# A hybrid attention and retention layer on one core: values freed by one cast and one subtraction, context units ahead of the values, summed weights made ahead, output weights in wider steps

## The chip, the cores and the metric

The kernel runs on one core of one Trainium2 chip. The metric is the device time of one execution in microseconds (us), as the median of several runs. The core has a matrix engine (TensorE, PE in the profile), a vector engine (VectorE, DVE), a scalar engine (ScalarE, ACT), GpSimd (POOL) and SyncE (SP), which issues most DMA transfers; ScalarE has a DMA queue of its own. Each engine takes its instructions in the order of the program and waits at each for what it needs.

## The reference

One backbone layer over 2048 latent tokens and 256 context tokens of width 1024, in float32:

```
h_lat = rmsnorm(x)*(1+scale)+shift;  h_ctx = rmsnorm(ctx)*(1+scale_c)+shift_c
[na_q|na_k|na_v|na_g|r_q|r_k|r_v|r_g] = h_lat @ w_in        # 8 groups of 512 columns
k_ctx, v_ctx, rk_ctx, rv_ctx          = the same columns of h_ctx @ w_in
o_na  = neighbourhood attention of 8 heads (8 x 16 window + all context keys, one softmax)
o_ret = forward + backward retention of 4 heads, scans started from the context's state
y     = concat(o_na*silu(na_g), head_rmsnorm(o_ret)*silu(r_g)) @ w_out
out   = rmsnorm(x + gate*y)
```

## The kernel before

Every float32 factor is held as a rounded part (hi, made by a cast on ScalarE) and a remainder (lo, made by a subtraction on VectorE or GpSimd), and each product is three products: hi by hi, hi by lo, lo by hi. The 2048 tokens of `h_lat` lie in four blocks of 512 (`blk[0]` to `blk[3]`, tiles `hhi` and `hlo`), the context in `blk[4]` (`chi`, `clo`). The order of the work is written out by hand; the part around the change goes so:

- Windows 0 to 4 compute the attention keys for one block each. A table `PLAN` says at which step each preparation stands. `spill_step` writes a piece of 512 KB of `h` to memory (`hS`); blocks 2 and 3 are spilled in windows 3 and 4, blocks 0 and 1 in the first Strassen part.
- A *unit* is a product of 256 tokens with 256 columns: 48 matmuls (line 365). `w_split` cuts 256 columns of weights from a raw tile `st` into `whi` and `wlo` (ScalarE line 336, line 338), two buffers each; `load_w` loads the next raw tile (SP, line 176), and two raw tiles fit.
- `u_v` is the unit of the attention values. It frees its result with two casts on ScalarE (line 405) and two subtractions on VectorE (line 406) into a tile `o` (two buffers), and writes eight pieces to `vB` (line 415), four from ScalarE's queue and four from SP's.
- `values` runs eight `u_v` units for two blocks. Between their steps `h_sums` makes sums of the blocks (`T`, lines 525 to 565), and after the fifth unit `w_sums` begins the first set of summed weights.
- `strassen` then runs six *sets* of 256 columns (gates and queries) over two blocks. A set is Strassen's scheme with seven products of 12 matmuls (line 623), in the order a11, a12, s4, a22, s2, s3, s1. `w_sums` makes the seven weights of the next set meanwhile (`cut`: ScalarE line 580, GpSimd line 581; sums on VectorE, lines 589 to 592) in functions `p0` to `p3`, which `step` calls after products 2, 4, 6 and 7; each writes into the buffers `whi` and `wlo` of the current set once that set's products have read them.
- The hooks of `strassen` are called at the same steps. In the second part they hold the work on the output weights: `wo_open`, eight `wo_gate` (a row of the gate: VectorE), `wo_row` (TensorE line 696), eight `wo_mul` (a multiplication on VectorE, line 700; two casts on ScalarE, line 704; two subtractions on GpSimd, line 705; four stores `woS` from ScalarE's queue, line 707; the next load `wraw` from SP, line 686).
- In the order of time: windows; two `u_v` units for the context; values of blocks 0 and 1; Strassen for 0 and 1; reload of blocks 3 and 2 from `hS` (16 loads, lines 756 and 760) beside four context units (`u_rk`, `u_rv`); values of blocks 3 and 2; Strassen for 2 and 3; a split of the first weights for the *fill* (retention units that go between attention steps); four fill units while the first head's data load; attention with fill; retention and output.

Of the kernel before, what the change touches and what calls it, by code (L numbers as in the profile page):

```python
# [11 lines left out]
F32R = mybir.dt.float32r  # L12
# [6 lines left out]
P = 128  # L19
# [63 lines left out]
def hybrid_kernel(ctx: ExitStack, tc: tile.TileContext, a: dict, out: bass.AP):  # L83
# [53 lines left out]
    def defer(n, fn):  # L137
        later.append([n, fn])
# [187 lines left out]
    def w_raw(c0):  # L326
        return st_halves(a["w_in"][:, c0:c0 + WG])
# [70 lines left out]

    def u_v(w, c0, tp):
        pm = yield from tokform(w, tp)  # L400
        vt = op.tile([P, 2, 2, 2, P], F32R, name="o")
        pv = pm.rearrange("p (t h e d) -> p t h e d", t=2, h=2, e=2)
        for e in range(2):
            hs, ls = slice(64 * e, 64 * e + 64), slice(64 - 64 * e, 128 - 64 * e)
            nc.scalar.copy(vt[:, :, :, e, hs], pv[:, :, :, e, :])
            nc.vector.tensor_tensor(vt[:, :, :, e, ls], pv[:, :, :, e, :], f(vt)[:, :, :, e, hs], ALU.subtract)
        s, o = (c0 - 1024) // WG, f(vt).rearrange("p t h e d -> p t (h e d)")
        if tp == 8:
            store(vS[s].rearrange("(t p) h d -> p t (h d)", p=P), o)
            return  # L410
        for e, j in enumerate(VORD):
            k0, cw = CWIN[j]
            dst = vB[s][:4 * cw, tp, e, :].rearrange("(t r c) d -> r c t d", t=2, r=2)
            for r, q in enumerate((nc.scalar, nc.sync)):
                defer(1 + r, lambda q=q, dst=dst[r], src=o[64 * r + k0:64 * r + k0 + cw]: q.dma_start(dst, src))
# [42 lines left out]
    for name, *args in LOADS:  # L458
        lds[name](*args)
    acts = dict(sq=squares, cs=lambda *i: colsum(*i), rs=lambda i: (rstd(i), spread_copy(i)), sp=lambda *i: spread(*i),  # L460
                mu=lambda i, u: spread_mul(i, (u,)), ab=prep_ab, hl=prep_hl, blk=alloc_blk, x=load_x, w=lambda: wr.append(w_raw(1024)),
                w2=lambda: load_w(), s=ada_split, m=ada_mm, ar=ada_row, af=ada_fin, p=prep_first,
                ws=lambda g: w01.append(w_split(wr[g], lo=WSL[g])))
    w01 = []
# [25 lines left out]
    def window(b):  # L490
        units = [u_k(w01, 512 + 256 * g, ct, b) for g in range(2) for ct in range(2)]
        left = [KC] * 4
        for n, u in enumerate(STEPS if b == 0 else [u for u in range(4) for _ in range(KC)]):
            if b == 4 and n == 16:
                wr.append(w_split(wr[2]))
            next(units[u])
            left[u] -= 1
            run_acts(32 * b + n)
            if b > 2 and n % 4 == 3:
                spill_step()  # L500
            if not left[u]:
                for _ in units[u]:
                    pass
                tick()
# [65 lines left out]
    def w_sums(rw):  # L570
        cut2 = lambda t: t.rearrange("p k w -> p (k w)").rearrange("p (s h k c) -> p s h k c", s=2, h=2, k=KH)
        a11, a21 = rw[0][:, :, 0:P], rw[0][:, :, P:WG]
        a12, a22 = rw[1][:, :, 0:P], rw[1][:, :, P:WG]
        W, tl = {}, {}

        def cut(key, n, s, r):
            if n not in tl:
                tl[n] = cut2(wa.tile([P, KC, WG], F32R, name=("whi", "wlo")[n % 2]))
            t = W[key] = tl[n][:, s]
            nc.scalar.copy(t[:, 0], r)  # L580
            nc.gpsimd.tensor_tensor(t[:, 1], r, f(t)[:, 0], ALU.subtract)  # L581

        def p0():
            cut("a11", 0, 0, a11)
            cut("a12", 0, 1, a12)

        def p1():
            cut("a22", 1, 0, a22)
            nc.vector.tensor_tensor(a22, a21, a22, ALU.add)
            nc.vector.tensor_tensor(a21, a11, a21, ALU.subtract)  # L590
            nc.vector.tensor_tensor(a11, a22, a11, ALU.subtract)
            nc.vector.tensor_tensor(a12, a12, a11, ALU.subtract)
# [12 lines left out]
    def plain_next(res):  # L605
        def p1():
            res.append(w_split(wcur.pop(0)))

        return [None, None, p1, None]

    def w_set(c0, W, T, A, B, ahead, hooks):
        isq = c0 < 512
# [28 lines left out]
        def step(n):  # L641
            tick()
            if ahead[n]:
                ahead[n]()
            if hooks:
                h = hooks.pop(0)
                if h:
                    h()

        V = nc.vector.tensor_tensor  # L650
# [76 lines left out]
    def values(ws, bb, hs, W):  # L727
        ahead = [None] * 4
        vu = [(w, c0, tp) for w, c0 in zip(ws, (1024, 1280)) for b in bb for tp in (2 * b, 2 * b + 1)]
        y = 0  # L730
        for n, (w, c0, tp) in enumerate(vu):
            for _ in u_v(w, c0, tp):
                y += 1
                if hs and y % 5 == 0:
                    hs.pop(0)()
            tick()
            if n == 4:
                W, ahead = w_sums(wcur.pop(0))
                ahead[0]()
        while hs:  # L740
            hs.pop(0)()
        ahead[2]()
        ahead[3]()
        return W

    load_w()
    w0, w1 = wr[3], w_split(wcur.pop(0))
    load_w()
    for w, c0 in ((w0, 1024), (w1, 1280)):
        unit(u_v(w, c0, 8))  # L750
    T = []
    W = values((w0, w1), (0, 1), h_sums(T, 0, 1), None)
    mid = []
    strassen(T, 0, 1, W, [spill_step] * 24, mid)
    for d in reload_parts(3):
        nc.sync.dma_start(*d)
    (wk0,) = mid
    load_w()
    for d in reload_parts(2):
        nc.sync.dma_start(*d)  # L760
    wk1 = w_split(wcur.pop(0))
    load_w()
    unit(u_rk(wk0, 2560, 8))
    wk2 = w_split(wcur.pop(0))
    load_w()
    unit(u_rk(wk1, 2816, 8))
    wk3 = w_split(wcur.pop(0))
    load_w()
    unit(u_rv(wk2, 3328, 8))
    w0 = w_split(wcur.pop(0))  # L770
    load_w()
    unit(u_rv(wk3, 3072, 8))
    w1 = w_split(wcur.pop(0))
    load_w()
    T = []
    W = values((w0, w1), (3, 2), h_sums(T, 2, 3), None)
    g = lambda k: lambda: wo_gate(k)
    m = lambda k: lambda: wo_mul(k)
    seq = [wo_open] + [g(k) for k in range(8)] + [None, wo_row] + [m(k) for k in range(8)]
    wo_steps = []  # L780
    for n, e in enumerate(seq):
        wo_steps += [e, None] if n in (2, 4, 6, 8) else [e]
    last = []
    strassen(T, 2, 3, W, wo_steps, last)
    w_next = last + [w_split(wcur.pop(0))]
    flush()

# [754 lines left out]
```

## Time and profile before

| | before |
|---|---|
| median of 3 runs | 1489.48 us (1488.07 to 1491.04) |
| the profiled execution's own time | 1491.74 us |
| its span | 1489.9 us |
| mean granted TensorE clock | 0.955 |
| TensorE busy | 1343.9 us (90%) |
| VectorE, ScalarE, GpSimd busy | 797.9, 594.5, 639.9 us |
| moved by DMA | 295.63 MB, mean 198 GB/s |

The profile is of one execution. The page gives busy times and the busy share in 40 slices of the span; a table of stretches gives busy time, granted clock and DMA share from one time to another; the timeline lists instructions with start, duration, and in brackets how long the engine was idle just before and what ended that. Matmuls overlap a little, so the distance from one start to the next tells their pace better than the duration.

### The profile page before, as it was taken

The page shows a single profiled execution, that of the slowest core. Times are in us where ns is not written, and L with a number is a line of the kernel's source. Part 1 is how long each engine was busy: PE and PEld are TensorE (multiplying, and loading weights), DVE is VectorE, ACT ScalarE, POOL GpSimd, SP SyncE. Part 2 cuts the span into 40 slices and gives each one's busy share as a digit, 9 for nine tenths or more (in the row PEclk, how much of TensorE's full clock was granted, in tenths as well). Part 3 has the DMA queues.
Part 4 walks back from the last instruction along what each step waited for, and adds up shares of the span by engine and source line. Part 5 has one row for each costly group of instructions (what it writes and reads, how often), then busy time and mean ns, then how long its engine had stood idle before and what let it go on. Part 6 is the DMA issues. An engine that isn't in the chain of part 4 may idle for free.

```text
span 1489.9 us, 23084 instructions
## 1 busy us (share of the span) xinstructions
PE 1343.9 (90%) x8236; PEld 1169.6 (79%) x8236; DVE 797.9 (54%) x1424; ACT 594.5 (40%) x1257; POOL 639.9 (43%) x593
## 2 busy tenths in 40 slices
PE   6999896999795889648999999999999989999997
PEld 2477795777694667448989988988999879888886
DVE  5776173334146353433777677777664554344435
ACT  5444122323322223224555654555564233333332
POOL 5342424433543434553545434435544134444442
PEclk9999997999797899779999999999999999999999
DMA  9445945455944534659776778997744898655533
GB/s 319 155 149 170 341 126 164 147 212 181 374 125 126 160 110 167 233 198 248 225 189 177 195 207 262 262 252 190 199 140 145 277 282 257 209 179 170 173 114 127
DMA packets 231764, 295.63 MB, mean 198 GB/s; under 512 B 17633, under 2 KB 172385, under 8 KB 230626
## 3 DMA queue, kind: packets, MB, share of 16 engines
q1 hardware_dynamic: 195842, 230.44, 51.9%
q10 hardware_dynamic: 35808, 63.72, 12.1%
q8 instruction: 66, 1.08, 0.3%
q14 instruction: 48, 0.39, 0.1%
HBM read 196.57 MB, written 97.52 MB: 197 GB/s over the span
## 4 chain that ended last, share of the span: by engine, by line
PE 44%; DMA 5%; DVE 4%; issue 3%; POOL 2%; ACT 2%; ACTq 0%; SPq 0%; DVEq 0%; POOLq 0%
PE mm L365 10%; PE mm L1386 10%; PE sS L947 4%; PE mm L354 4%; PE tr L974 3%; PE po L995 3%; PE mm L1109 2%; PE tr L976 2%; PE po L997 2%; DMA v<-rvS 1%; PE mm L1298 1%; PE mm L1297 1%; PE mm L1296 1%; PE mm L1277 1%; DMA rvS<-o 1%
## 5 line engine op out<-in xcount | busy, mean ns | idle before, releaser
L365 PE MATMUL mm<-whi,hhi 128*128 128x256 f32 x768 | 225.7, 294 | 19.2 <-ACT whi L336 19.2
L365 PE MATMUL mm<-wlo,hhi 128*128 128x256 f32 x768 | 218.4, 284 | 2.0 <-POOL wlo L338 2.0
L365 PE MATMUL mm<-whi,hlo 128*128 128x256 f32 x768 | 217.9, 284 | 0.0
L978 ACT CAST pt<-tr 128x640 fp32r<-128x640 f32 (+1 forms) x128 | 95.6, 747 | 170.2 <-PE tr L976 167.7
L365 PEld LDWEIGHTS mm<-whi,hhi 128*128 128x128 f32 x768 | 147.7, 192 | 19.7 <-ACT whi L336 19.7
L984 DVE TENSOR_TENSOR pt<-tr,pt 128x640 fp32r<-128x640 f32 (+1 forms) x128 | 113.9, 890 | 77.6 <-ACT pt L978 76.2
L967 POOL TENSOR_SCALAR sp<-sp,stt 128x640 f32<-128x640 f32 (+2 forms) x128 | 103.1, 808 | 113.2 <-DVE stt L966 80.8
L365 PEld LDWEIGHTS mm<-wlo,hhi 128*128 128x128 f32 x768 | 147.2, 192 | 2.6 <-POOL wlo L338 2.6
L365 PEld LDWEIGHTS mm<-whi,hlo 128*128 128x128 f32 x768 | 147.9, 193 | 0.0
L338 POOL TENSOR_TENSOR wlo<-st,whi 128x256 fp32r<-128x256 f32 (+1 forms) x87 | 102.9, 1197 | 87.1 <-ACT whi L336 74.6
L956 DVE CUSTOM_DVE_ANT_0 sp<-sS,nb 128x640 f32<-128x640 f32 (+2 forms) x128 | 105.6, 825 | 40.7 <-DMA nb<-in_rpb_t_dram 27.3
L961 ACT ACTIVATE sp<-sp,stt 128x640 f32<-128x640 f32 (+2 forms) x128 | 107.4, 839 | 26.1 <-DVE stt L956 25.0
L623 PE MATMUL mm<-hhi,wlo 128*128 128x512 f32 x240 | 78.4, 443 | 43.1 <-ACT wlo L580 28.4
L623 PE MATMUL mm<-hhi,whi 128*128 128x512 f32 x336 | 99.8, 406 | 14.9 <-ACT whi L580 7.5
L947 PE MATMUL sS<-k,q 128*128 128x256 f32 (+3 forms) x512 | 99.4, 316 | 10.6 <-DVE stt L956 5.4
L581 POOL TENSOR_TENSOR wlo<-st,wlo 128x512 fp32r<-128x512 f32 x36 | 49.7, 1396 | 137.1 <-ACT wlo L580 137.1
L354 PE MATMUL mm<-hhi,whi 128*128 128x512 f32 x256 | 107.7, 421 | 0.0
L354 PE MATMUL mm<-hlo,whi 128*128 128x512 f32 x256 | 101.7, 397 | 5.7 <-DVE hlo L255 2.2
L354 PE MATMUL mm<-hhi,wlo 128*128 128x512 f32 x256 | 101.7, 397 | 0.3 <-DVE wlo L338 0.3
L623 PEld LDWEIGHTS mm<-hhi,wlo 128*128 128x128 f32 x240 | 49.1, 209 | 64.2 <-ACT wlo L580 33.2
L1386 PE MATMUL mm<-wor,y 128*128 128x512 f32 x384 | 95.7, 398 | 1.7 <-DVE xt L1395 1.1
L947 PEld LDWEIGHTS sS<-k,q 128*128 128x128 f32 x512 | 83.3, 189 | 17.2 <-DVE stt L956 8.1
(253 smaller groups left out, 3110.1 us busy)
## 6 DMA issues: line engine op xcount, KB each, us to landing
st<-in_w_in_dram SPq DMA_DIRECT2D x64, 512.0 KB
q<-qS SPq DMA_DIRECT2D x64, 256.0 KB
k<-kS SPq DMA_DIRECT2D x16, 576.0 KB
kS<-o SPq DMA_DIRECT2D x16, 512.0 KB
hS<-hhi SPq DMA_DIRECT2D x16, 512.0 KB
hS<-hlo SPq DMA_DIRECT2D x16, 512.0 KB
qS<-o ACTq DMA_DIRECT2D x16, 512.0 KB
hhi<-hS SPq DMA_DIRECT2D x16, 512.0 KB
```

What stands on the lines that cost most here:

```text
L338: eng.tensor_tensor(l, r, f(h), ALU.subtract)
L354: nc.tensor.matmul(pm[:, :n], ww[:, k, cs], h[:, k, :], start=(k == 0 and i == 0), stop=(k == KC - 1 and i == 2))
L365: nc.tensor.matmul(pm[:, t * WG:(t + 1) * WG], h[:, k, o:o + P], ww[:, k, :], start=(k == 0 and i == 0), stop=(k == KC - 1 and i == 2))
L581: nc.gpsimd.tensor_tensor(t[:, 1], r, f(t)[:, 0], ALU.subtract)
L623: nc.tensor.matmul(pm, ww[:, k, :], hh[:, k, :], start=(k == 0 and i == 0), stop=(k == KH - 1 and i == 2))
L947: nc.tensor.matmul(o, hd["q"][i][:, hl, j * P:(j + 1) * P], k, start=(hl == 0), stop=(hl == 1))
L956: nc.vector.tensor_tensor_reduce(T["sp"][:, :n], T["s"], nbz[big][:, o:o + n], -1.0, 3e38, ALU.add, ALU.min, T["st"][:, 0:1])
L961: nc.scalar.activation(sp[:, :n], sp[:, :n], AF.Exp, bias=st[:, 0:1], scale=-1.0, accum_out=st[:, 1:2])
L967: nc.gpsimd.tensor_scalar(sp[:, :n], sp[:, :n], st[:, 2:3], 0.0, ALU.mult, ALU.add)
L978: nc.scalar.copy(pt[:, :ng_ + 2, 0, :], tr[:, :ng_ + 2, :])
L984: nc.vector.tensor_tensor(pt[:, :n, 1, :], tr[:, :n, :], f(pt)[:, :n, 0, :], ALU.subtract)
L1386: nc.tensor.matmul(pm, yy[:, k, :], ww[:, k, sl], start=(k == 0 and i == 0), stop=(k == 3 and i == 2))
```

## The change

- `u_v`: the tile's parts are laid out so that one cast and one subtraction over all 512 columns do it; all eight stores `vB` go from SP's queue.
- The four context units `u_rk` and `u_rv` (`CTXU`) now stand right behind the windows, ahead of the two context `u_v` units. Blocks 2 and 3 are spilled in windows 2 and 3. The reload of blocks 3 and 2 has no unit beside it any more.
- `w_sums`: other sums in another order (five VectorE operations instead of four); `p0` makes a11, a12 and the first four sums, `p1` (after product 4) s4 and a22, `p2` s2 and s3, `p3` s1. In `values` `p0` and `p1` stand after the fifth and sixth unit. The split of plain weights behind the last set stands at step 1 instead of step 2, with one remainder half on VectorE.
- The output weights: `wo_open`, the eight `wo_gate` and `wo_row` stand in the first Strassen part, every second step; the eight `wo_mul` in the second, every third step.

```diff
     def u_v(w, c0, tp):
         pm = yield from tokform(w, tp)
-        vt = op.tile([P, 2, 2, 2, P], F32R, name="o")
-        pv = pm.rearrange("p (t h e d) -> p t h e d", t=2, h=2, e=2)
-        for e in range(2):
-            hs, ls = slice(64 * e, 64 * e + 64), slice(64 - 64 * e, 128 - 64 * e)
-            nc.scalar.copy(vt[:, :, :, e, hs], pv[:, :, :, e, :])
-            nc.vector.tensor_tensor(vt[:, :, :, e, ls], pv[:, :, :, e, :], f(vt)[:, :, :, e, hs], ALU.subtract)
+        vt = op.tile([P, 4, 4, 64], F32R, name="o")
+        pv = pm.rearrange("p (g e d) -> p g e d", e=2, d=64)
+        nc.scalar.copy(vt[:, :, ::3, :], pv)
+        nc.vector.tensor_tensor(vt[:, :, 1:3, :], pv, f(vt)[:, :, ::3, :], ALU.subtract)
...
-            for r, q in enumerate((nc.scalar, nc.sync)):
-                defer(1 + r, lambda q=q, dst=dst[r], src=o[64 * r + k0:64 * r + k0 + cw]: q.dma_start(dst, src))
+            for r in range(2):
+                defer(1 + r, lambda dst=dst[r], src=o[64 * r + k0:64 * r + k0 + cw]: nc.sync.dma_start(dst, src))
...
-    wseq = [1280, *SETS, 2560, 2816, 3328, 3072, 1024, 1280, *SETS, fseq[0][1], fseq[1][1]]
+    CTXU = [(2560, u_rk), (2816, u_rk), (3328, u_rv), (3072, u_rv)]
+    wseq = [2816, 3328, 3072, 1024, 1280, *SETS, 1024, 1280, *SETS, fseq[0][1], fseq[1][1]]
...
-            if b > 2 and n % 4 == 3:
+            if b in (2, 3) and n % 4 == 3:
                 spill_step()
...
         def p0():
             cut("a11", 0, 0, a11)
             cut("a12", 0, 1, a12)
+            V(a11, a11, a21, ALU.subtract)
+            V(a12, a12, a22, ALU.subtract)
+            V(a12, a12, a11, ALU.add)
+            V(a21, a21, a22, ALU.add)
 
         def p1():
-            cut("a22", 1, 0, a22)
-            nc.vector.tensor_tensor(a22, a21, a22, ALU.add)
-            nc.vector.tensor_tensor(a21, a11, a21, ALU.subtract)
-            nc.vector.tensor_tensor(a11, a22, a11, ALU.subtract)
-            nc.vector.tensor_tensor(a12, a12, a11, ALU.subtract)
-            cut("s2", 1, 1, a11)
+            cut("s4", 1, 0, a12)
+            cut("a22", 1, 1, a22)
+            V(a22, a22, a11, ALU.subtract)
 
         def p2():
-            cut("s4", 3, 0, a12)
+            cut("s2", 2, 0, a22)
+            cut("s3", 2, 1, a11)
 
         def p3():
-            cut("s3", 2, 1, a21)
-            cut("s1", 2, 0, a22)
+            cut("s1", 3, 0, a21)
             load_w()
 
-        return W, [p0, None, lambda: (p1(), p2()), p3]
+        return W, [p0, p1, p2, p3]
...
+    for c0, u in CTXU:
+        wn = w_split(wcur.pop(0), lo=1)
+        load_w()
+        unit(u(w0, c0, 8))
+        w0 = wn
...
+    hooks = [[spill_step] if n < 16 else [] for n in range(24)]
+    for n, e in enumerate([wo_open] + [g(k) for k in range(8)]):
+        hooks[2 * n + 1].append(e)
+    hooks[22].append(wo_row)
     mid = []
-    strassen(T, 0, 1, W, [spill_step] * 24, mid)
-    for d in reload_parts(3):
-        nc.sync.dma_start(*d)
+    strassen(T, 0, 1, W, hooks, mid)
+    for b in (3, 2):
+        for d in reload_parts(b):
+            nc.sync.dma_start(*d)
+    w0, w1 = mid + [w_split(wcur.pop(0), lo=1)]
...
-    seq = [wo_open] + [g(k) for k in range(8)] + [None, wo_row] + [m(k) for k in range(8)]
...
+    for k in range(8):
+        hooks[3 * k].append(m(k))
```

What moves on the engines shows best at two places. The first is ScalarE from the last two value units to the first products of the Strassen part (`o<-mm` is the freeing of a unit, `vB` its stores, `whi<-st` and `wlo<-st` the summed weights, the last row the freeing of the first product). Before:

```order
L405 CAST o<-mm 128x4x64 x2
L415 DMA vB_68<-o 32x2x512 x2
L415 DMA vB_68<-o 24x2x512 x2
L405 CAST o<-mm 128x4x64 x2
L415 DMA vB_68<-o 32x2x512 x2
L415 DMA vB_68<-o 24x2x512 x2
L580 CAST wlo<-st 128x512 x3
L580 CAST whi<-st 128x512 x2
L652 COPY o_1960<-mm 128x512
```

After:

```order
L579 CAST whi<-st 128x512 x2
L524 CAST hhi<-o_1919 128x512
L403 CAST o<-mm 128x4x2x64
L579 CAST wlo<-st 128x512 x2
L524 CAST hhi<-o_1919 128x512
L403 CAST o<-mm 128x4x2x64 x2
L579 CAST whi<-st 128x512 x2
L579 CAST wlo<-st 128x512
L653 COPY o_2189<-mm 128x512
```

The stores have left ScalarE, and the casts of s4 and a22 (`wlo`) stand ahead of the freeing of the last two units instead of behind it. The second place is SP at the end of the reload behind the first Strassen part (`hhi<-hS`, `hlo<-hS` are the last of its 16 loads, `st` are raw weights in halves of a tile, `vB` the first stores of the next values). Before:

```order
L760 DMA hhi<-hS_0_91 128x1024
L760 DMA hlo<-hS_1_92 128x1024
L176 DMA st<-in_w_in_dram 128x4x256 x10
L415 DMA vB_67<-o 32x2x512 x2
L415 DMA vB_67<-o 24x2x512 x2
```

After:

```order
L771 DMA hhi<-hS_0_91 128x1024
L771 DMA hlo<-hS_1_92 128x1024
L176 DMA st<-in_w_in_dram 128x4x256 x4
L413 DMA vB_67<-o 32x2x512 x2
L413 DMA vB_67<-o 24x2x512 x2
```

Between the reload and the next values' first store stand two weights' loads instead of five, and the load that stood between block 3's eight pieces and block 2's is gone.

More of the change, by code (lines that the diff above doesn't have):

```diff
@@ L645, in step @@
             if hooks:
-                h = hooks.pop(0)
-                if h:
+                for h in hooks.pop(0):
                     h()
@@ L738, in values @@
                 W, ahead = w_sums(wcur.pop(0))
-                ahead[0]()
+            if n in (4, 5):
+                ahead[n - 4]()
         while hs:
@@ L746, in hybrid_kernel @@
     load_w()
[L747 removed]
+    w0 = wr[3]
+    for c0, u in CTXU:
[3 more added lines that the diff above has]
+        w0 = wn
+    w1 = w_split(wcur.pop(0), lo=1)
     load_w()
@@ L750, in hybrid_kernel @@
         unit(u_v(w, c0, 8))
+    g = lambda k: lambda: wo_gate(k)
+    m = lambda k: lambda: wo_mul(k)
     T = []
     W = values((w0, w1), (0, 1), h_sums(T, 0, 1), None)
+    hooks = [[spill_step] if n < 16 else [] for n in range(24)]
+    for n, e in enumerate([wo_open] + [g(k) for k in range(8)]):
+        hooks[2 * n + 1].append(e)
+    hooks[22].append(wo_row)
     mid = []
-    strassen(T, 0, 1, W, [spill_step] * 24, mid)
-    for d in reload_parts(3):
-        nc.sync.dma_start(*d)
-    (wk0,) = mid
-    load_w()
[L759 to L773, printed above, removed]
+    strassen(T, 0, 1, W, hooks, mid)
[3 more added lines that the diff above has]
+    w0, w1 = mid + [w_split(wcur.pop(0), lo=1)]
+    load_w()
     load_w()
@@ L776, in hybrid_kernel @@
     W = values((w0, w1), (3, 2), h_sums(T, 2, 3), None)
-    g = lambda k: lambda: wo_gate(k)
-    m = lambda k: lambda: wo_mul(k)
-    seq = [wo_open] + [g(k) for k in range(8)] + [None, wo_row] + [m(k) for k in range(8)]
-    wo_steps = []
-    for n, e in enumerate(seq):
-        wo_steps += [e, None] if n in (2, 4, 6, 8) else [e]
+    hooks = [[] for n in range(24)]
+    for k in range(8):
+        hooks[3 * k].append(m(k))
     last = []
-    strassen(T, 2, 3, W, wo_steps, last)
+    strassen(T, 2, 3, W, hooks, last)
     w_next = last + [w_split(wcur.pop(0))]
```

9 lines of the change are left out of this document (5 added, 4 removed).

## The prediction

> **What bounds the kernel now.** I read the head of the page, then a table of stretches, then TensorE's timeline at each gap, then the other engines there. First the span, TensorE's busy tenths in 40 slices of 37 us, and its granted clock in the same slices:
>
> ```profile
> span 1489.9 us, 23084 instructions
> PE   6999896999795889648999999999999989999997
> PEclk9999997999797899779999999999999999999999
> ```
>
> TensorE is the bound (mostly 9s), but slices 4 to 18 show holes with the clock down at 7. The change works there. I cut that time where TensorE's kind of product changes; a row has the stretch, its length, busy time with count for PE, PEld, DVE, ACT and POOL, granted clock, DMA share and GB/s:
>
> ```profile
> 163.87:184.30 20.43, 13.79 (x97) 13.32 (x98) 2.55 (x6) 5.96 (x10) 13.75 (x6) 0.83 1.01 368
> 184.30:230.30 46.00, 46.00 (x386) 46.00 (x385) 33.32 (x35) 13.12 (x23) 13.82 (x8) 1.00 0.44 134
> 230.30:372.87 142.57, 123.34 (x506) 95.73 (x504) 53.54 (x79) 42.16 (x76) 55.88 (x44) 0.94 0.52 180
> 372.87:411.90 39.03, 28.70 (x188) 27.78 (x189) 6.22 (x6) 13.07 (x15) 24.01 (x10) 0.78 0.99 365
> 411.90:458.64 46.74, 46.74 (x390) 46.53 (x388) 28.22 (x25) 11.84 (x18) 19.12 (x8) 1.00 0.39 116
> 458.64:633.43 174.79, 136.06 (x508) 104.23 (x508) 74.36 (x95) 50.50 (x92) 78.88 (x56) 0.85 0.50 163
> 633.43:685.30 51.87, 25.59 (x192) 24.83 (x193) 12.85 (x14) 13.44 (x20) 21.03 (x16) 0.78 0.67 216
> sum 521.43, PE 420.22 PEld 358.42 DVE 211.06 ACT 150.09 POOL 226.50; mean PE 60.03 PEld 51.20 DVE 30.15 ACT 21.44 POOL 32.36
> ```
>
> The stretches are two context units, eight value units, Strassen, four context units, eight value units, Strassen, and from its last product to the first attention product with four fill units in it. Only the two value stretches run without a hole at clock 1.00: 46.00 / 8 = 5.75 us a unit. The pace of Strassen products is the distance of two starts:
>
> ```profile
> 584.39 2.97 PE L623 MATMUL mm<-hlo,wlo 128*128 128x512 f32 x12
> 587.20 2.97 PE L623 MATMUL mm<-hhi,wlo 128*128 128x512 f32 x12
> 571.65 1.88 PE L696 MATMUL mm<-gacc,one 128*128 128x512 f32 x4
> ```
>
> 2.81 us a product, 42 products 118.0; the gate's row adds 1.9 once. So the stretches need 11.5 + 46 + 118 + 23 + 46 + 119.9 + 23 = 387.4 of their 521.4 us. The other 134 are waits and the slow clock behind them. The waits:
>
> ```profile
> 168.88 0.58 PE L365 MATMUL mm<-whi,chi 128*128 128x256 f32 x1 [5.01 <-ACT whi L336]
> 248.56 0.79 PE L623 MATMUL mm<-hhi,wlo 128*128 128x512 f32 x1 [12.45 <-ACT wlo L580]
> 316.28 0.72 PE L623 MATMUL mm<-hhi,wlo 128*128 128x512 f32 x2 [1.09 <-POOL wlo L581]
> 466.17 0.80 PE L623 MATMUL mm<-hhi,whi 128*128 128x512 f32 x1 [7.53 <-ACT whi L580]
> 485.27 0.79 PE L623 MATMUL mm<-hhi,wlo 128*128 128x512 f32 x1 [10.70 <-ACT wlo L580]
> 511.54 0.73 PE L623 MATMUL mm<-hhi,wlo 128*128 128x512 f32 x2 [2.11 <-POOL wlo L581]
> 512.43 1.05 PE L623 MATMUL mm<-hhi,wlo 128*128 128x512 f32 x2
> 513.28 0.63 PE L623 MATMUL mm<-hlo,wlo 128*128 128x512 f32 x1
> 605.76 0.77 PE L623 MATMUL mm<-hhi,whi 128*128 128x512 f32 x1 [7.20 <-ACT g L704]
> 652.66 0.58 PE L365 MATMUL mm<-whi,hhi 128*128 128x256 f32 x1 [19.23 <-ACT whi L336]
> 685.30 1.25 PE L947 MATMUL sS<-k,q 128*128 128x288 f32 x4 [5.02 <-DMA vt<-vB]
> ```
>
> Nearly all wait for weights that ScalarE and GpSimd have not yet cut. A wait costs more than itself: behind the 2.11 us at 511.54 two matmuls take 0.85 (512.43 to 513.28), 0.43 each against 2.81 / 12 = 0.23, for about 4 us until 515.42, so 1.8 us more.
>
> **The change part by part.** *Context units ahead, spills earlier.* The first context product waits because ScalarE's cast of its weights stands behind the freeing of keys, which waits for key stores that share the DMA with the spills:
>
> ```profile
> 163.81 0.37 ACT L374 CAST o<-mm 128x256 fp32r<-128x256 f32 x1 [3.77 <-DMA kS<-o]
> 167.78 1.99 ACT L336 CAST whi<-st 128x1024 fp32r<-128x1024 f32 x2
> ```
>
> With no spill in window 4 half of the 20.43 - 11.5 = 8.9 us over should go; I take 4.5, between 0 and 8.9. Window 2 gets eight spills that window 3 already bore; I cost them at nothing, since TensorE has six result buffers before a late key store stops it; if preparation falls behind, about one wait like those here, 3 us, comes on top. Each of the six units needs a split (2.0 on ScalarE; one subtraction on GpSimd, half of the 4.78 for two below, the other on VectorE) against 5.75 on TensorE, so the rest is covered, and the four units lose the reload that now fills the DMA beside them (share 0.99). Sum: 34.5 + 4.5 = 39.0 for 59.5.
>
> *Values, and their joint to Strassen.* Freeing one unit holds ScalarE from 224.92 to 228.73, and the casts of s4 stand behind the last one:
>
> ```profile
> 224.92 0.37 ACT L405 CAST o<-mm 128x256 fp32r<-128x256 f32 x1
> 225.78 0.37 ACT L405 CAST o<-mm 128x256 fp32r<-128x256 f32 x1 [0.49 <-DVE o L406]
> 226.64 2.09 ACTq L415 DMA_DIRECT2D vB<-o  x4
> 242.99 0.62 ACT L580 CAST wlo<-st 128x512 fp32r<-128x512 f32 x1 [2.20 <-DMA vB<-o]
> 253.31 2.34 SPq L415 DMA_DIRECT2D vB<-o  x4
> ```
>
> One cast of 512 columns (0.62) replaces 3.8 us: 3.2 us less, eight times per stretch, at no gain on TensorE inside the stretch (no hole there) but with the block sums and s4, a22 done before it ends. s2, s3, s1 must still wait for the last unit to give up its weights; three casts and three subtractions, about 2 + 3 x 1.3 (half of the 2.51 at 247.86 below) = 6 us, against four products = 11.2. So the joints cost 0; bound 5 if VectorE's block sums run late. The four extra stores on SP take 2.34: 4.7 in 5.75 us, nothing else queued there; the unit after next needs the tile 11.5 us later.
>
> *Weights three products ahead.* s4 is now cut after product 4 and read 5 products = 14 us later; ahead lie two casts, two subtractions and four sums, about 7 us. The 1.1 to 2.1 us per set with its slow clock goes. The fifth sum is 0.69 us (the row at 247.16 below) in sets where VectorE is less than half busy (53.54 in 142.57). One set's loss may stay in each part. Gates in the first part: a wait on VectorE for their rows was
>
> ```profile
> DVE wraw L700 <- DMA wraw<-in_w_out_dram: 35.5, 6, 8.2
> 247.16 0.69 DVE L592 TENSOR_TENSOR st<-st 128x512 f32<-128x512 f32 x1
> 247.86 2.51 POOL L581 TENSOR_TENSOR wlo<-st,wlo 128x512 fp32r<-128x512 f32 x2 [2.91 <-ACT wlo L580]
> ```
>
> at most 8.2 us; gates now come every 3 or 4 products (8.4 or 11.2 us), multiplications every 5 or 6 (14 us). SP is shared by 16 spills, gates and weights; a load of weights holds the next gate's row until GpSimd has cut s1, about 6 us into the next set, still one step ahead. First part: 118 + 1.9 + 1.6 = 121.5 (119.9 to 128.3, six times 1.4 left); second: 118 + 1 = 119 (to 126.4). The 7.20 and the two stalls after it go with the wider steps.
>
> *Reload with nothing beside it.* This is what comes late next. SP reaches the reload here:
>
> ```profile
> 364.35 0.46 SPq L756 DMA_DIRECT2D hhi<-hS  x1
> ```
>
> 8.5 us before the end of the part. 16 loads are 8.4 MB, 23 us at 365 GB/s: block 3 is in at +3 to +5, block 2 at +15 to +18. TensorE wants block 3's last quarter at +2 and block 2 at +11.5. I take 6 us of waiting and slow clock: 52 (46 if loads keep ahead; 59 if the DMA is as full as in 372.87:411.90).
>
> *End of the second part.* The first fill weights are cut after product 4, so fill starts at once: 23 us. But the heads' loads stand on SP behind the load whose buffer the second weights' cut frees:
>
> ```profile
> 656.03 0.68 DVE L668 TENSOR_TENSOR o<-mm,o 128x512 f32<-128x512 f32 x1
> 663.48 2.00 ACT L336 CAST whi<-st 128x1024 fp32r<-128x1024 f32 x2 [5.15 <-DMA woS<-g]
> 664.61 4.78 POOL L338 TENSOR_TENSOR wlo<-st,whi 128x1024 fp32r<-128x1024 f32 x2 [2.85 <-ACT whi L336]
> 669.41 0.93 SPq L176 DMA_DIRECT2D st<-in_w_in_dram  x2
> ```
>
> From the last additions (656.03) to the cast 7.4, about 5 without the `woS` stores between; 5.9 to SP; 15.9 to attention (685.30): 27 after the last product. Between 23 and 36.
>
> Sum: 39 + 46 + 121.5 + 52 + 119 + 27 = 404.5 for 521.4, 117 less. Against the profiled execution's 1491.74 that is 1374.7; its time stands 2.3 above the runs' median 1489.48, so **1373**. All lower ends give 387.4 (1356), all upper ends about 449 (1417).
>
> [...]
>
> **The rivals.** *Reload held until the part's last product.* Speaks for it: SP stands behind weights; against: 364.35. Then block 3 is in at +13.5, block 2 at +25: 16 us instead of 6, 1383.
>
> *The joints stay late.* The change would not do what it says there, because s4's sums queue on VectorE behind block sums: 33.32 of 46.00 us busy at the first joint speaks for it, the freed ScalarE against. 10 us at both joints: 1393.
>
> *Slower: the stores on SP.* All 128 value stores queue on SP; once an issue takes over 5.75 / 8 = 0.72 us, tiles come free late and TensorE goes at SP's pace. To eat 117 us the 16 units must take 7.3 us more each: 1.63 us an issue. 2.34 / 4 = 0.59 speaks against. At 1.7 us: 13.6 a unit, 126 us lost, 1499.
>
> **How the numbers follow.** My forecast 0.72 (own range 1356 to 1390), reload 0.12, joints 0.12, SP 0.02, smaller mixtures 0.02. The range 1357 to 1400 holds the first three but for their tails. Within 0.2% (3 us) is what measurement cannot tell from no change; only 117 us lost elsewhere would land there: 0.01. Faster 0.97, slower 0.02.
>
> **What would show it.** Right: no idle over 3 us on TensorE between the first context unit and the fill; sets of 19.7 us; clock 1.00 in the Strassen parts; a wait for `hS` loads at the second values; a wait of about 4 us before attention. Wrong: waits for `wlo` at the first sets, for `vB` in the values, or a reload wait over 10 us.

## The result and the profile after

The changed kernel took 1448.84 us (median of 4 runs, 1446.62 to 1451.75) against 1489.56 for the kernel before on the same chip: a ratio of 0.9728 (95% interval 0.9706 to 0.9750). It is faster by 41 us, not by 117: outside the range, on its slow side. From the head of the page, the span, TensorE's busy tenths and its granted clock:

```profile
span 1450.0 us, 23128 instructions
PE   6989899889898787789999999999999999999997
PEclk9999899999989898999999999999999999999999
```

The holes of the first half are shallower, but there are still holes. The table of stretches, cut as in the prediction (now six context units; eight value units; Strassen; eight value units; Strassen; the fill up to the first attention product):

```profile
165.49:210.24 44.75, 37.74 (x288) 37.45 (x289) 13.96 (x10) 15.93 (x21) 23.29 (x9) 0.89 0.67 219
210.24:256.31 46.07, 46.07 (x387) 46.07 (x386) 34.83 (x30) 11.69 (x16) 15.13 (x8) 1.00 0.44 110
256.31:392.20 135.89, 123.12 (x506) 97.16 (x505) 69.50 (x86) 42.15 (x74) 57.18 (x43) 0.96 0.68 221
392.20:450.70 58.50, 52.92 (x390) 50.60 (x388) 45.81 (x36) 15.49 (x23) 23.14 (x10) 0.91 0.75 255
450.70:612.40 161.70, 127.45 (x499) 99.70 (x500) 66.78 (x88) 49.14 (x88) 76.44 (x59) 0.90 0.54 170
612.40:645.90 33.50, 25.04 (x198) 24.09 (x197) 10.52 (x12) 10.16 (x15) 11.46 (x11) 0.96 0.73 219
```

| stretch | before | forecast | after | missed by |
|---|---|---|---|---|
| context units (six) | 59.46 | 39.0 | 44.75 | 5.8 |
| values 1 | 46.00 | 46.0 | 46.07 | 0.1 |
| Strassen 1 | 142.57 | 121.5 | 135.89 | 14.4 |
| values 2 | 46.74 | 52.0 | 58.50 | 6.5 |
| Strassen 2 | 174.79 | 119.0 | 161.70 | 42.7 |
| to attention | 51.87 | 27.0 | 33.50 | 6.5 |
| sum | 521.43 | 404.5 | 480.41 | 75.9 |

Three quarters of the miss lie in the two Strassen parts. The longest of TensorE's waits there, from its timeline:

```profile
284.36 0.47 PE L625 MATMUL mm<-hhi,whi 128*128 128x512 f32 x1 [3.69 <-DVE o L660]
310.11 0.77 PE L625 MATMUL mm<-hhi,whi 128*128 128x512 f32 x1 [4.46 <-DVE o L660]
...
487.62 0.76 PE L625 MATMUL mm<-hhi,whi 128*128 128x512 f32 x1 [7.76 <-DVE o L660]
...
538.09 0.76 PE L625 MATMUL mm<-hhi,whi 128*128 128x512 f32 x1 [3.64 <-ACT g L705]
567.02 0.76 PE L625 MATMUL mm<-hhi,whi 128*128 128x512 f32 x1 [7.91 <-DVE o L660]
609.35 1.22 PE L625 MATMUL mm<-hhi,wlo 128*128 128x512 f32 x2 [5.76 <-ACT o L653]
```

In the kernel before nearly every wait was for weights (`whi`, `wlo`). Those waits are gone except at the joints, where a Strassen part begins. In their place TensorE waits for what empties its result buffers: the additions on VectorE (line 660) and the copy of a set's first product on ScalarE (line 653). The row at 538.09 names ScalarE's cast of `g`, but no matmul reads `g`. Line 660 had ended at 537.93, 0.16 us ahead, as it ended 0.15 us ahead of the row at 567.02; so this wait is of the same kind, and the profile only names what came last. Lines of the changed kernel in what follows: 653 the copy of the first product into `yb`, 654 `V(xa)`, 660 to 664 the additions that free s2, s3, a22 and s4; 579 and 580 a weight's cast (ScalarE) and remainder (GpSimd); 587 to 590 the four sums of `p0`, 595 the sum `V(a22, a22, a11)` at the end of `p1`; 701, 705, 706 and 708 an output weight's multiplication, casts, remainders and stores.

The set before the wait at 567.02 shows how it comes about, from the timelines of ScalarE, GpSimd and VectorE (ACTq is ScalarE's sequencer issuing DMAs):

```profile
558.17 1.14 ACT L705 CAST g<-wraw 128x512 fp32r<-128x512 f32 x2 [5.79 <-DVE wraw L701]
558.92 2.49 POOL L706 TENSOR_TENSOR g<-wraw,g 128x512 fp32r<-128x512 f32 x2 [4.40 <-issue]
560.22 1.57 ACTq L708 DMA_DIRECT2D woS<-g  x3
562.38 1.14 ACT L579 CAST wlo<-st 128x512 fp32r<-128x512 f32 x2 [2.53 <-POOL g L706]
563.07 2.48 POOL L580 TENSOR_TENSOR wlo<-st,wlo 128x512 fp32r<-128x512 f32 x2 [1.66 <-ACT wlo L579]
565.59 0.69 DVE L595 TENSOR_TENSOR st<-st 128x512 f32<-128x512 f32 x1 [7.45 <-POOL wlo L580]
566.19 0.68 DVE L660 TENSOR_TENSOR o<-mm,o 128x512 f32<-128x512 f32 x1
```

VectorE stands idle 7.45 us at line 595. That sum overwrites a22 in place, so it must wait until GpSimd has read a22 for its remainder. GpSimd waits for ScalarE's casts; ScalarE stands at the stores `woS`, which need GpSimd's remainders of the output weights (done at 561.41). Behind line 595 on VectorE stand the additions that free products. TensorE's products share six result buffers (the pool `pp` of the kernel), all of them still full here, so the second product of the next set cannot start: TensorE is idle for 7.91 us, until the first addition (line 660) has run. VectorE kept the order of the program here: the product that line 660 reads had ended at 550.73 (547.76 + 2.97 in TensorE's timeline) and the copy of line 653 at 551.34, yet line 660 starts at 566.19, 0.60 us after line 595.

The totals of VectorE's waits in the second part:

```profile
DVE o L654 <- ACT o L653: 43.8, 5, 13.6
DVE st L595 <- POOL wlo L580: 27.2, 6, 7.9
```

A wait of the same kind was to be seen in the second part of the kernel before, six times and up to 3.7 us long; but there the additions stood ahead of it:

```profile
DVE st L589 <- POOL wlo L581: 16.8, 6, 3.7
525.94 0.68 DVE L663 TENSOR_TENSOR o<-mm,o 128x512 f32<-128x512 f32 x1
529.16 0.69 DVE L589 TENSOR_TENSOR st<-st 128x512 f32<-128x512 f32 x1 [2.54 <-POOL wlo L581]
```

The change moved the sum from behind product 6 to behind product 4, ahead of the additions.

### The profile page after: what moved, and what is told of

The parts are those of the page before. It is cut to its first block, busy times and chain, and to the rows that moved or that the text cites. A ratio compares the mean times of both kernels' runs of the same rounds, so it can differ in the third digit from the quotient of the medians.

```text
span 1450.0 us, 23128 instructions
## 1 busy us (share of the span) xinstructions
PE 1338.7 (92%) x8236; PEld 1167.1 (80%) x8236; DVE 828.2 (57%) x1426; ACT 589.1 (41%) x1239; POOL 620.9 (43%) x585
## 4 chain that ended last, share of the span: by engine, by line
PE 44%; DMA 5%; DVE 4%; issue 3%; POOL 3%; ACT 2%; SPq 0%; ACTq 0%; POOLq 0%; DVEq 0%
PE mm L1383 10%; PE mm L365 10%; PE sS L944 5%; PE mm L354 4%; PE tr L971 3%; PE po L992 3%; PE tr L973 2%; PE po L994 2%; PE mm L1106 2%; DMA v<-rvS 1%; DMA k<-kS 1%; PE mm L1295 1%; PE mm L1294 1%; PE mm L1293 1%; PE mm L1274 1%
## 5 line engine op out<-in xcount | busy, mean ns | idle before, releaser
L625 PE MATMUL mm<-hhi,whi 128*128 128x512 f32 x336 | 107.5, 421 | 35.3 <-DVE o L660 27.5
L338 POOL TENSOR_TENSOR wlo<-st,whi 128x256 fp32r<-128x256 f32 (+1 forms) x79 | 83.8, 1072 | 98.9 <-ACT whi L336 78.1
L625 PEld LDWEIGHTS mm<-hhi,whi 128*128 128x128 f32 x336 | 67.4, 202 | 56.3 <-issue 30.3
L354 PE MATMUL mm<-hhi,whi 128*128 128x512 f32 x256 | 108.3, 423 | 0.0
L354 PE MATMUL mm<-hhi,wlo 128*128 128x512 f32 x256 | 102.5, 400 | 0.2 <-DVE wlo L338 0.2
L580 POOL TENSOR_TENSOR whi<-st,whi 128x512 fp32r<-128x512 f32 x48 | 66.4, 1404 | 78.3 <-ACT whi L579 51.5
L1392 DVE TENSOR_TENSOR xt<-mm,xt 128x512 f32<-128x512 f32 x64 | 43.8, 687 | 85.0 <-PE mm L1383 79.5
```

Of the source, the lines that this page charges most:

```text
L338: eng.tensor_tensor(l, r, f(h), ALU.subtract)
L354: nc.tensor.matmul(pm[:, :n], ww[:, k, cs], h[:, k, :], start=(k == 0 and i == 0), stop=(k == KC - 1 and i == 2))
L625: nc.tensor.matmul(pm, ww[:, k, :], hh[:, k, :], start=(k == 0 and i == 0), stop=(k == KH - 1 and i == 2))
```

## The experiments

Four theories of the lost 76 us, with one experiment each: T1, the sum `V(a22)` on VectorE ahead of the freeing additions; T2, the single result tile `o3` of a set, whose store must land before the next set's copy; T3, the stores `woS` that hold ScalarE; T4, the 64 value stores on SP. T1 to T3 are links of one loop. The next set's products need freed buffers. The additions that free them stand on VectorE behind the sum of line 595, that sum waits for GpSimd, GpSimd waits for ScalarE's casts, and ScalarE may stand at its own stores or at the copy of line 653, which waits for the store of a result tile of the set before. So the question was also whether the three are one wait or several. Then came combinations, and single parts of the change by themselves. Four kernels ran in a group; the kernel before took 1492.95, 1490.42 and 1491.77 us beside the three groups, so ratios are compared. The parts are cut here from their first product to the first product of the next kind, which puts the changed kernel at 136.98 and 163.00 us.

| kernel | us | ratio to before (95%) | Strassen 1 | Strassen 2 |
|---|---|---|---|---|
| changed kernel | 1448.84 | 0.9728 (0.9706 to 0.9750) | 136.98 | 163.00 |
| V(a22) a step later | 1427.12 | 0.9560 (0.9543 to 0.9576) | 125.03 | 155.00 |
| one `o3` for a part | 1428.60 | 0.9575 (0.9559 to 0.9591) | 125.68 | 152.87 |
| `woS` from SP | 1427.74 | 0.9568 (0.9544 to 0.9591) | 139.46 | 140.93 |
| half of `vB` from ScalarE | 1464.15 | 0.9812 (0.9794 to 0.9829) | 142.80 | 169.30 |
| all three edits | 1392.93 | 0.9349 (0.9335 to 0.9363) | 124.95 | 125.23 |
| V(a22) later, `woS` from SP | 1403.85 | 0.9416 (0.9391 to 0.9442) | 123.76 | 128.22 |
| old order of sums | 1455.74 | 0.9774 (0.9754 to 0.9793) | 153.29 | 154.42 |
| old output-weight steps | 1457.46 | 0.9783 (0.9761 to 0.9805) | 128.43 | 168.28 |
| before + new values | 1483.27 | 0.9942 (0.9924 to 0.9960) | 138.82 | 187.94 |
| before + context units ahead | 1485.80 | 0.9954 (0.9934 to 0.9974) | | |
| old sums, other two edits | 1446.04 | 0.9694 (0.9666 to 0.9723) | 154.34 | 148.18 |
| all three, head's loads first | 1388.75 | 0.9300 (0.9266 to 0.9333) | | |

**V(a22) a step later** (T1).

```diff
         def p1():
...
-            V(a22, a22, a11, ALU.subtract)
         def p2():
+            V(a22, a22, a11, ALU.subtract)
             cut("s2", 2, 0, a22)
```

> The last sum of a set's weights (s2 = a22 - a11 on VectorE) stands after the additions that free the products, instead of ahead of them; nothing else differs from the changed kernel. Theory 1 (that sum waits for GpSimd's cut of a22, and the freeing of s2, s3, m4 and m3 waits behind it on VectorE, so TensorE runs out of result buffers): the waits of TensorE for the freeing of s2 (11.4 us in the first Strassen part, 16.2 in the second) and the slow clock behind them go, 30 to 45 us faster than the changed kernel, about 1410. Theory 2 (the one result tile of a set whose store must land before the next set may begin to free): under 10 us. Theory 3 (the output weights' stores hold ScalarE): 10 to 20 in the second part alone, none in the first.

Measured: 25 us less than the changed kernel by the ratios (0.0168 of 1490), a little under the 30 to 45 that T1 gave. The second part keeps long waits, now mostly for line 653, the copy that waits for the result tile (TensorE's waits of that part in all, their count, the longest):

```profile
PE mm L625 <- ACT o L653: 11.3, 5, 7.1
```

So T1 is shown for the first part, where it took 12 us, and is one cause of several in the second.

**One result tile for a whole part** (T2). As one tile, only its half that is stored waits for the store; allocated anew, all of it did, the copy into `yb` too. In the changed kernel that copy reads:

```profile
526.46 0.59 ACT L653 COPY o<-mm 128x512 f32<-128x512 f32 x1 [6.76 <-DMA gS<-o]
```

```diff
+    obt = {}
...
-            o = env["st"].tile([P, 2, 512], F32R, name="o3", bufs=1) if extra else op.tile([P, 2, 512], F32R, name="o")
+            o = obt["t"] if extra else op.tile([P, 2, 512], F32R, name="o")
...
     def strassen(T, A, B, W, hook, last):
+        obt["t"] = env["st"].tile([P, 2, 512], F32R, name="o3", bufs=1)
```

> The fourth result tile of a set is one tile for all six sets of a part, so that the freeing of a set's first product waits for the landing of the store of that half only which it overwrites (none for the four gate sets). Theory 2 (landing of this store holds the next set): ScalarE's waits for gS stores at the freeing of the first product go, 20 to 35 us faster than the changed kernel. Theory 1 (VectorE's order): at most 8 us, since the additions still wait for GpSimd. Theory 3: at most 8 us.

Measured: 23 us less, in both parts. Most of what is left is T1's wait (both parts together; line 662 is line 660 of the changed kernel):

```profile
PE mm L627 <- DVE o L662: 18.1, 4, 8.0
```

**The output weights' stores from SP** (T3).

```diff
-                defer(1, lambda hl=hl, sl=sl, w=w: nc.scalar.dma_start(woS[hl][k, :, sl], f(w)[:, hl, :]))
+                defer(1, lambda hl=hl, sl=sl, w=w: nc.sync.dma_start(woS[hl][k, :, sl], f(w)[:, hl, :]))
```

> The 32 stores of the output weights go from SP's queue instead of ScalarE's. Theory 3 (ScalarE stands at these stores until GpSimd has made the remainder, ahead of the casts of s4 and a22): 15 to 25 us faster than the changed kernel, all in the second Strassen part. Theory 1: 5 to 10 us, since the casts come some 2 to 4 us earlier in four of six sets. Theory 2: under 5 us.

Measured: 24 us less, all of it in the second part (there are no such stores in the first, which was 2.5 us longer).

**Half of the value stores from ScalarE again** (T4).

```diff
-            for r in range(2):
-                defer(1 + r, lambda dst=dst[r], src=o[64 * r + k0:64 * r + k0 + cw]: nc.sync.dma_start(dst, src))
+            for r, q in enumerate((nc.scalar, nc.sync)):
+                defer(1 + r, lambda q=q, dst=dst[r], src=o[64 * r + k0:64 * r + k0 + cw]: q.dma_start(dst, src))
```

> Half of the value stores go from ScalarE's queue again, as in the kernel before; the single cast and subtraction stay. Theory 4 (64 stores on SP are late, so that the first set of each Strassen part waits 7.3 and 6.2 us on VectorE for its tile): 8 to 15 us faster than the changed kernel. Theories 1 to 3: within 4 us of it; if ScalarE at the stores is what held the kernel before at the joints, up to 10 us slower.

Measured: 12.5 us slower. T4 falls as a cost; moving the stores to SP was a gain. Four of them hold ScalarE for 1.73 us here (2.03 or 2.04 in each of the four groups before), and the next cast waits for that, with TensorE behind it:

```profile
273.13 1.73 ACTq L413 DMA_DIRECT2D vB<-o  x4
274.89 1.14 ACT L579 CAST whi<-st 128x512 fp32r<-128x512 f32 x2 [2.52 <-DMA vB<-o]
275.56 0.79 PE L625 MATMUL mm<-hhi,whi 128*128 128x512 f32 x1 [5.44 <-ACT whi L579]
```

**All three edits together.**

> Three edits at once on the changed kernel: V(a22) moved from the second piece of the weights' sums to the third, one result tile ob for a whole Strassen part, and the output weights' stores issued by SP. In the changed kernel the first Strassen part took 135.9 us and the second 161.7; with the first edit alone 125.0 and 155.0, with the second alone 125.7 and 152.9, with the third alone 139.5 and 140.9. Loop theory (VectorE, ScalarE and GpSimd wait for each other round a ring within each set, and each edit cuts one link of it): the rest goes as well, first part 120 to 123, second 120 to 126, so 1390 to 1405 us against 1493 before. Rival (the three edits remove one and the same 22 us): 1418 to 1430. What is left above 118 to 120 a part is then not this ring.

Measured: 1392.93 us, 56 less than the changed kernel, inside what the loop theory said in total; the first part lies 2 us above what it gave for it, the second within it. Page and stretches:

```profile
PE   6989899999998999899999999999999999999997
PEclk9999899999999999899999999999999999999999
253.59:378.54 124.95, 120.88 (x510) 96.32 (x509) 74.69 (x89) 42.33 (x74) 61.89 (x43) 0.99 0.77 252
378.54:431.61 53.07, 49.29 (x385) 47.90 (x384) 40.73 (x34) 15.55 (x22) 23.20 (x9) 0.97 0.75 255
431.61:556.84 125.23, 119.90 (x507) 95.45 (x505) 73.96 (x88) 50.40 (x89) 80.05 (x60) 0.99 0.69 217
```

The stretches tell more than the theories did. In the first part the first edit saves 12.0, the second 11.3, and all three 12.0: one wait, and either link cut removes it. In the second they save 8.0, 10.1 and 22.1, together 37.8: nearly the sum, 40.2. So the rival (one and the same wait) is true of the first part and false of the second. That the sum fits is partly chance, though: the next run shows that the links do not simply add up.

**Without the second edit.**

> Two of the three edits, V(a22) a step later and the output weights' stores on SP; the result tile ob is still one whose store must land before the next set. Loop theory: first part 125 as with the first edit alone, second part 125 to 135, so 1398 to 1412 us. If the result tile is the link that counts once the other two are gone, the second part stays at 140 and the time at 1415 to 1425.

Measured: 1403.85 us, as the loop theory said; the second part took 128.22. In the second part the first and third edit together save 34.8 us, more than 8.0 and 22.1 make, and the second adds only 3.0 to that, not 10.1. So the links hang together there too, and which of them holds which set was not taken apart. Over the whole kernel the result tile is worth 10 us by the ratios (0.9416 against 0.9349); the profiled executions differ by 6.1, of which 1.8 lie in the two parts.

**The old order of the sums in the changed kernel.** `w_sums` is that of the kernel before (its `p0` and the list of its four pieces), all else is changed.

> The changed kernel with the weights' sums of the kernel before (five sums in its second and third pieces, s1 and s3 cut in the fourth, all eight summed weights in the old order); everything else stays changed. The forecast's account, in which cutting the weights earlier was worth the two waits at the joints (16 and 18 us) and 1 to 2 us a set: 1485 to 1500 us. Loop theory, in which the new order of the sums took the waits for weights away and put as many waits for result buffers in their place: 1455 to 1475.

Measured: 7 us slower (0.9774 against 0.9728), at the lower end of what the loop theory gave and far from the forecast's account. As made, the part of the change on which the forecast's largest terms rested was worth 7 us: it saved 16 us in the first part and cost 9 in the second.

**The old order of the sums with the other two links cut.** The edits of the second and third experiment on top of the one just shown.

> The changed kernel with the old order of the weights' sums, and the two other links of the ring cut: one result tile ob per part, output weights' stores on SP. Loop theory (the sums' new order is worth something only once the ring is cut, since then its waits for weights are all that is left): the 2.1 us waits with slow clock in most sets and some 9 us at each joint stay, parts of 140 to 150 us, 1425 to 1440, against 1393 with the new order and V(a22) a step later. Rival (the new order is worth nothing in itself, 4 us as in the uncut kernel): 1395 to 1405.

Measured: 1446 us, 6 above the range expected. TensorE's waits that are left in the first part are for weights alone, as in the kernel before: 14.3 us for casts (five waits, the longest 8.5) and 8.6 for remainders (six, the longest 2.1).

Against 0.9349 that makes the new order worth 51 us once nothing stands in its way (with its own sum a step later), and 7 us when the loop does.

**The old steps for the output weights.** All 18 in the second part, at the steps they had in the kernel before.

> The changed kernel with the output weights' steps where they were before, all 18 in the second Strassen part (the gate's eight steps one or two products apart, then the eight multiplications one product apart). The first part is then free of the gate's steps and loses its row product of 1.9 us. Forecast's account: the 7.2 us wait and two short ones come back, 8 to 12 us slower, 1460 to 1465. Loop theory: eight multiplications with sixteen casts and stores in consecutive products hold ScalarE for most of two sets, so up to 20 us slower: 1465 to 1475. No change (1450 to 1455) if the steps only move waits from set to set.

Measured: 8 us slower (0.9783 against 0.9728), with intervals that just part, and with a time between those that the accounts gave. The first part was 8.6 us shorter and the second 5.3 longer; from the second part to the first attention product it took 39.9 us (609.25 to 649.16 in its timeline) instead of 32.2. The wider steps so gained mostly where the fill's weights are cut, behind the part.

**Two parts of the change by themselves on the kernel before.** First the values freed by one cast and one subtraction, with all `vB` stores on SP; then the context units ahead of the values with the spills and the reload as in the change.

> The kernel before with one part of the change: values freed by one cast and one subtraction, and all their stores issued by SP. Forecast's account (ScalarE's copying of values held the cuts at both joints, waits of 12.5 and 7.5 + 10.7 us with slow clock behind them): 25 to 30 us faster, 1460 to 1465. Other account (the changed kernel with the old sums still waited 8.5 and 8.9 us at the joints, so the freeing was only a part of these waits): 8 to 15 us faster, 1475 to 1482.

> The kernel before with one part of the change: the four context units moved ahead of the values, spills a window earlier, both blocks reloaded at the end of the first Strassen part. Forecast's account: 20.5 us less in the context units, 5 us more in the second values for the reload, so 1474 to 1477. By the stages of the changed kernel as measured (14.7 us less in the context units, 11.8 us more in the second values): 1485 to 1488, nearly nothing.

Measured: 0.9942 and 0.9954, 9 and 7 us, both near what the second account of each gave. With the values alone the wait at the first joint went from 12.45 to 8.37 us and the two at the second from 7.53 and 10.70 to 3.59 and 8.90: the freeing was the smaller part of those waits. The second part stayed at 187.94 (186.49 before, cut so). Moving the context units gains little, in part because some of it comes back in the second values, which took 58.28 us to the next part's first product against 54.27 before.

**All three edits, and the head's loads ahead of the fill's third weights.**

```diff
     wseq += [c0 for _, c0 in fseq[2:]]
-    load_w()
...
     load_v(heads[0], (0, 1, 2))
+    load_w()
```

> The three edits together (1393 us), and the load of the third fill weights issued behind the first head's loads instead of ahead of them. In the three edits' trace SP stood at that load until 571.47, when GpSimd's cut gave its buffer free; the head's loads followed from 572.52, and TensorE waited 6.93 us for vt at 586.95. If that load is what makes them late: the wait goes, 1385 to 1388. If the head's own six loads of vt (10.27 us on SP) set it: 2 us or less, 1391 to 1393.

In the three edits' trace SP and TensorE read:

```profile
571.47 0.93 SPq L176 DMA_DIRECT2D st<-in_w_in_dram  x2
576.01 10.27 SPq L926 DMA_DIRECT2D vt<-vB  x6
586.95 0.58 PE L947 MATMUL sS<-k,q 128*128 128x288 f32 x1 [6.93 <-DMA vt<-vB]
```

Measured: 0.9300 against 0.9349, about 7 us faster, and no wait ahead of the first attention product, which starts at 582.46. The load that stood in front was the cause. This is the fastest version: 1388.75 us (1384.71 to 1394.62), by the ratios 64 us under the changed kernel.

## Why the prediction was wrong

The mechanism was right that cutting the weights earlier removes the waits for weights: of the long waits named in the prediction the first (5.37 us now) and the last (7.03) stayed, and the others for weights are 2.3 us or less. The step that failed stands under "Weights three products ahead": "The fifth sum is 0.69 us [...] in sets where VectorE is less than half busy". It took the sums at their duration and put nothing behind them. But the fifth sum waits for GpSimd, and what is queued behind it frees TensorE's buffers. The busy share said nothing on that; a list of what stands behind each moved instruction on its engine would have. In its place the runs showed a sum that waits 17.6 us (six waits) in the first part and 27.2 (six) in the second, and a loop behind it that cost 12 us in the one and 37.8 in the other. The sign named for being right, no idle of TensorE over 3 us, failed seven times in the two parts. The trace of before had the row (16.8 us in six waits at line 589), ahead of nothing that TensorE needed.

It also had, once, the very thing that failed. The prediction lists 7.20 us at 605.76 among the waits that go with the wider steps, by a row that names ScalarE's cast of `g`. VectorE reads there, in the kernel before and then ahead of the 3.64 us in the changed one:

```profile
603.78 1.23 DVE L700 TENSOR_TENSOR wraw<-wraw,gacc 128x1024 f32<-128x1024 f32 x1 [5.67 <-DMA wraw<-in_w_out_dram]
604.92 0.68 DVE L659 TENSOR_TENSOR o<-mm,o 128x512 f32<-128x512 f32 x1
...
535.51 0.69 DVE L595 TENSOR_TENSOR st<-st 128x512 f32<-128x512 f32 x1 [2.80 <-POOL wlo L580]
537.25 0.68 DVE L660 TENSOR_TENSOR o<-mm,o 128x512 f32<-128x512 f32 x1
```

Before, the multiplication of line 700 waited for its row, and the first addition that frees a buffer (line 659) stood behind it; TensorE started 0.16 us after that addition ended. So it was a wait for a buffer already then. By terms:

- *Strassen 1, 121.5 forecast, 135.89.* With the three edits 124.95 (cut 1.1 us later than in the prediction's table): 12 us of the miss were the loop; some 2 are the cuts at the joint, 2.20 and 0.62 us of waiting.
- *Strassen 2, 119 forecast, 161.70.* With the three edits 125.23. 37.8 us were the loop, most of it through the stores `woS` on ScalarE (22.1 by themselves). "The 7.20 and the two stalls after it go with the wider steps" came true in so far as no multiplication waits for its row any more and the two stalls are gone. But the wider steps put one or two multiplications into every set, each with two casts and four stores, and the 3.64 us at 538.09 are the loop's: line 660 stands there behind the waiting sum and one multiplication. The 4 to 5 left are waits of 0.70, 2.29, 1.19 and 0.62 at the joint and the slower pace behind them (0.43 us from one matmul to the next at 443.26).
- *Values 1, 46 forecast, 46.07.* Right.
- *Values 2, 52 forecast, 58.50.* Waits for `hS` loads came, as said (the longest 2.00 us, at 397.10). From its first product to the next part's first product the stretch took 57.44 us, and 53.07 with the three edits, so some 4 of the 6.5 us went with the loop; by which wait was not tried.
- *Context units, 39 forecast, 44.75.* "With no spill in window 4 half of the 8.9 us over should go": none went.

```profile
169.49 0.37 ACT L374 CAST o<-mm 128x256 fp32r<-128x256 f32 x1 [3.31 <-DMA kS<-o]
170.86 0.58 PE L365 MATMUL mm<-whi,chi 128*128 128x256 f32 x1 [5.37 <-ACT whi L336]
```

  ScalarE still waits for key stores at the end of window 4. The spills did not leave that window as the program's order suggests:

```profile
139.24 13.67 SPq L176 DMA_DIRECT2D st<-in_w_in_dram  x4
159.32 2.59 SPq L487 DMA_DIRECT2D hS<-hlo  x2
```

  SP stood 13.67 us at the loads of raw weights, and six spills that stand in window 3 in the program were issued behind them, from 152.97 to 161.91. TensorE was in window 4 from 153.94 on, and the key stores went out between and behind these spills. So the step "no spill in window 4" did not hold. That these spills make the key stores late was not tried.
- *To attention, 27 forecast, 33.50.* The place was right (the head's loads behind a weight load on SP) and its size too small: the wait was 7.03 us, not 4, and the reordering removed it.

Of the rivals, "the joints stay late" (1393) looked to the right engine and the wrong place: the waits at the joints were 0.4 to 2.3 us each, and VectorE was late in the sets instead. "The stores on SP" met its condition and not its price:

```profile
217.53 57.22 SPq L413 DMA_DIRECT2D vB<-o  x60
275.86 8.18 SPq L413 DMA_DIRECT2D vB<-o  x4
275.88 0.69 DVE L654 TENSOR_TENSOR o<-mm,o 128x512 f32<-128x512 f32 x1 [7.28 <-DMA vB<-o]
```

60 stores in 57.22 us are 0.95 us each, over the 0.72 at which it was to decide, and the last four came 2.05 us apart, 28 us after the last unit. Yet the value units ran without a hole; VectorE's wait of 7.28 us in the next part's first set is where the late stores show, as one more link of the loop. The split queue was 12.5 us slower all the same.

With the three edits the time is 20 us above the forecast, of which the terms place some 18: about 6 at the context units, 2 and 5 in the two parts, 1 in the values, 4 ahead of attention. So 1373 was 20 us too low even for a kernel with the loop cut.

## What to carry to other kernels

Before a small operation is costed at its duration, write down what it must wait for where it now stands and which instructions wait behind it on its engine; an in-place update waits for every reader of the old value, as line 595 did for GpSimd, 17.6 us in the first part and 27.2 in the second. An order that makes one producer earlier is worth only what the other links of the loop let through: here the same edit gave 7 us with them and 51 without. Where several edits each save the same amount, run them together and in pairs: in one stretch they were the same wait, in another the three savings seemed to add up, and the pair showed that they did not. And where a row names an engine whose result the waiting one does not read, look for what ended just before.

## What the runs showed of the hardware

A short wait did not always slow TensorE. In the run with all three edits:

```profile
267.44 0.74 PE L627 MATMUL mm<-hhi,whi 128*128 128x512 f32 x2 [2.20 <-ACT whi L579]
268.80 4.05 PE L627 MATMUL mm<-hhi,whi 128*128 128x512 f32 x10 [0.62 <-POOL whi L580]
272.69 2.97 PE L627 MATMUL mm<-hlo,whi 128*128 128x512 f32 x12
```

Behind 2.20 and 0.62 us of idle ten matmuls took 3.89 us (0.39 apart), then the pace is 0.23 again. Behind 1.04 us alone, at 301.70 in the same run, two took 0.47 (302.24 to 302.71), 0.23 apart, so nothing was lost; the forecast charged the waits of 1.1 us with the slow clock as well. The length of a wait alone does not decide it. In the changed kernel:

```profile
374.79 0.47 PE L625 MATMUL mm<-hhi,whi 128*128 128x512 f32 x1 [2.75 <-DVE o L660]
375.32 0.63 PE L625 MATMUL mm<-hhi,whi 128*128 128x512 f32 x2
375.79 0.39 PE L625 MATMUL mm<-hlo,whi 128*128 128x512 f32 x1
```

Behind 2.75 us of idle two matmuls took 0.47, 0.23 apart, while the 2.11 us of the prediction's rows were followed by 0.43 a matmul. So the slower pace followed once on 2.11 us of idle and once did not follow on 2.75 us. What decides between them was not tried.
